# Two pairs of gate tiles at each layer end by seven half-size products, and another order of these products

## The chip, the core and the metric

The kernel runs on one core of a Trainium2 chip. The metric is the device time of one execution in microseconds (us), of the slowest core where there are several; here there is one. Lower is better. The engines are named as in the profile: PE multiplies matrices (PEld loads its weights), DVE is the vector engine, ACT the scalar engine, POOL is GpSimd, SP issues most DMAs. Each engine works through its own queue in the order in which the program writes it.

## The reference

A trunk of four layers works on 512 prompt rows and 8 sample rows together, 520 columns in the kernel. Every layer has another mixer (mLSTM, short convolution, dilated attention, pooling). The change touches what follows each mixer:

```python
def per_layer_embed(x, p, pe_w, pg_w):
    gate = jax.nn.sigmoid(x @ pg_w)
    return x + gate * (p.astype(x.dtype) @ pe_w)

x = x + mixer(rms_norm(x))          # ends with "@ w_out", the out projection
x = per_layer_embed(x, p[i], pe_w[i], pg_w[i])
```

Here x is 520 x 1024, pg_w is 1024 x 1024, p is 520 x 256. All is float32.

## The kernel before

**Numbers.** Activations lie transposed: eight tiles x[0..7] of 128 features x 520 columns. Every float32 operand is split into a high part, which PE takes as it is, and a low part, the rest; a product is high*high + low*high + high*low, so three matmuls for each block of 128 x 128 weights. `mm6` (L328) does one such block for all columns, in two halves of 256 and 264: six matmuls. `proj` (L410) does one output tile of 128 features: eight blocks, 48 matmuls.

**Weights.** A weight tile of 128 x 1024 is loaded by SP into one of four buffers `wf`. "high" copies it on ACT into one of four buffers `wh` (L255), "low" subtracts on DVE, wl = wf - wh (L264). For the names in MOVED (w_b and w_bo, the convolution's weights) the low part of a single tile, or of the first tile of a pair, is made otherwise: ACT writes -wh into `wl` (L260), and a DMA issued by POOL adds the weights from memory onto it (L262).

**Order.** Nothing is reordered at run time. `plan` (L60) lists the weight tiles in the order of use as Items with a cost in planned us (0.12 for a matmul). `due` (L114) goes through them once and gives each step a due time: "high" of an item is due when the earliest of the four `wh` buffers comes free, where an item holds its buffer from then until its begin plus cost (or plus `life`). While the program writes matmuls, `pump` (L289) moves a clock on by 0.72 for each `mm6` and 1.44 for each product of `seven`, and writes every weight step that has come due into its engine's queue right there. So the due time sets behind which other instructions of ACT, DVE and POOL a weight step stands. `item` (L308) sets the clock to the begin of the item that is taken.

**Seven products.** In the convolution two output tiles of 128 features for 520 columns are made together as a 2 x 2 block product by `seven` (L341): seven half-size products of 12 matmuls with 260 columns each, 84 in place of 96. For that POOL forms sums of the weights of a pair ("sum", four operations, L276 to L279), whose high and low parts ("hs", "ls", 512 wide) come from ACT and DVE, and sums of the activations are made once (`summed`, L568, POOL operations at L582 to L585). The products stand in PE's queue in the order 1 to 3, then what is still open of the pair before (`flush`), then 4 to 6; the seventh (`last`, L370) waits as the next thing to flush, in the next `seven` after its third product or in the next `proj` after its fourth block.

**Layer end.** `out_proj` (L613) adds the mixer's result to x[j], tile by tile, and splits x[j] into high and low parts (`xs`). Then `embed` (L632) runs over j = 0..7: 12 matmuls for p @ pe_w into `pe` (a weight tile w_pe serves four j), 48 for x @ pg_w into `pg` (w_pg), then the end of the tile: sigmoid on ACT (L647), two multiplications with `pe` (L649) and the addition to x[j] (L650) on DVE, the split for the next layer (ACT L469, DVE L470; in the last layer one copy on ACT), a square on ACT (L517) and its addition on DVE (L518). The weight steps that come due while a tile's matmuls are written follow in the queues. In planned us of this stage, tile j begins at 7.2 j, and a w_pe tile holds its buffer for 28.8. The last tile of the last layer is made in `final` (L661).

**Streams.** Work beside the matmuls is written as generators in streams; `tick`, every second block of a `proj`, moves each by one step.

Of the kernel before, what the change touches and what calls it, by code (L numbers as in the profile page):

```python
# [8 lines left out]
F32 = mybir.dt.float32  # L9
# [5 lines left out]
P = 128  # L15
# [24 lines left out]
NPLAIN = 3  # L40
HALF = T // 2
FBUFS, HBUFS, SBUFS = 4, 4, 4
MOVED = ("w_b", "w_bo")


# [14 lines left out]
def plan():  # L60

    out = []
    add = lambda *key, **kw: out.append(Item(key, **kw))

    def end(i, name, halves, begun=False):
        cs = range(2 if halves else 1)
        for c in cs:
            for j in range(2):
                if c or not begun:
                    last = c == len(cs) - 1 or i == 1  # L70
                    add(name, j, *([c] if halves else []), life=(2 - j) * 5.76 if last else None)
        for j in range(2, KD):
            for c in cs:
                add(name, j, *([c] if halves else []))
        for j in range(KD):
            if j % 4 == 0:
                add("w_pe", i, j // 4, cost=0, life=28.8)
            add("w_pg", i, j, cost=7.2)

    for hd in range(H):  # L80
        for j in (hd, 8 + hd, 16 + 2 * hd, 17 + 2 * hd, 32 + 2 * hd, 33 + 2 * hd):
            add("w_a", j)
    for j in range(16):
# [24 lines left out]
    for m in range(2):  # L108
        add("w_grp", 3, m)
    end(3, "w_do", True, True)  # L110
    return out


def due(items):  # L114
# [17 lines left out]
    for i, it in enumerate(items):  # L132
        it.begin = t
        if len(it.keys) == 1:
            ld = min(slots["wf"])
            sp = at(max(ld, take("wh", t + (it.life or it.cost))), i, "high")
            low = at(sp + 1.3, i, "low")
            at(take("wf", low + 2) - 0.01, i, "load")
        else:
            ld, ld2 = sorted(slots["wf"])[:2]  # L140
            one = at(max(ld, ld2, t - 12.8), i, "sum")
            h1 = at(max(ld, take("wh", t + 5.76), t - 14.4), i, "high")
            h2 = at(max(ld2, take("wh", t + 10.08), one + 6.6), i, "high2")
# [51 lines left out]
class Net:  # L195
# [47 lines left out]
    def make(self, i, op):  # L243
# [7 lines left out]
        new = lambda tag, n=1024, pool=None, dt=F32R: (pool or self.wp).tile([P, n], dt, tag=tag, name=self.nm(tag))  # L251

        def high(k, tag, n=1024, pool=None):
            t["h" + k] = new(tag, n, pool)
# [83 lines left out]
            mm(out[j], wl, a[0][:, PARTS[j]], start=False, stop=stop)  # L338
        self.pump(0.72)

    def seven(self, keys, B, dst, done):  # L341

# [51 lines left out]
        step()  # L394
        self.pend = last

# [216 lines left out]
    def out_proj(self, name, y, i, begun=None):  # L613

        nc = self.nc
        xs = []
        first = begun or self.proj_pair(name, y, 8 if i == 2 else 16)
        self.pt = [self.act() for _ in range(2)]
        for k in range(2):
            nc.sync.dma_start(self.pt[k], self.d["pT"][i, k])  # L620
        for j in range(KD):
# [8 lines left out]
        return xs  # L630

    def embed(self, i, xs):  # L632

        nc, d = self.nc, self.d
        hs, we = [], None
        g0 = C_NG + (i + 1) * KD
        for j in range(KD):
            if j % 4 == 0:
                we = self.weights("w_pe", i, j // 4)
# [3 lines left out]
            if i == 3 and j == KD - 1:  # L643
                return self.final(xs, pe, hs)
            pg = self.proj("w_pg", i, j, a=xs)
            sg = self.act()
            nc.scalar.activation(sg, pg, AF.Sigmoid)  # L647
            for u in range(2):
                nc.vector.tensor_mul(sg[:, PARTS[u]], self.part(pe, u), sg[:, PARTS[u]])  # L649
            nc.vector.tensor_add(self.x[j], self.x[j], sg)  # L650
            if i < 3:
                hs.append(self.split(self.x[j], self.col(g0 + j)))
            else:
                hs.append(self.act())
                nc.scalar.activation(hs[j], self.x[j], AF.Copy, scale=self.col(C_FG + j))
            self.square_in(j)
        self.sums = {} if i == 0 else None
        self.finish_norm(hs, g0, 3, *((4, 1), (2, 3), (0, 0))[i], sums=self.sums)
        return hs

    def final(self, xs, pe, xg):  # L661
# [8 lines left out]
        xg.append(self.act())  # L670
# [46 lines left out]
    def mlstm(self, h, lay):  # L717
# [3 lines left out]
        with ExitStack() as st:  # L721
# [53 lines left out]
            while main.gens or samp.gens:  # L775
                zs.append(self.scaled(self.proj("w_a", 48 + len(zs), a=h)))
        ex = lay.enter_context(tc.tile_pool(name="mly", bufs=16))
        self.streams = [self.gate]
        y = []
        for j, z in enumerate(zs):  # L780
# [271 lines left out]
    def conv(self, h, lay):  # L1052
# [4 lines left out]
        with ExitStack() as st:  # L1057
# [88 lines left out]
            self.look = 4  # L1146
            nc.sync.dma_start(d["o_conv_p"], po)
            nc.sync.dma_start(d["o_conv_s"], so)
        return y


    def attention(self, h, lay):
# [49 lines left out]
            gate()  # L1202

        self.finish = finish
        return y

    def rope(self, t, cs, out=None, keep=0):
# [237 lines left out]
    def pooling(self, h, lay):  # L1445
# [3 lines left out]
        with ExitStack() as st:  # L1449
# [22 lines left out]
            self.grouped(3, *last, y)  # L1472
            nc.sync.dma_start(d["o_pool_p"], pp)
            nc.sync.dma_start(d["o_pool_s"], sp[:, :, 1:16])
        return y, first

    def grouped(self, g, rr, zs, y):
# [40 lines left out]
    def run(self):  # L1518
# [32 lines left out]
        for i, (mixer, w) in enumerate(  # L1551
            ((self.mlstm, "w_ao"), (self.conv, "w_bo"), (self.attention, "w_co"), (self.pooling, "w_do"))
        ):
            with ExitStack() as lay:
# [4 lines left out]
            h = self.embed(i, xs)  # L1559


OUTS = {
# [124 lines left out]
```

## Time and profile before

| | us |
|---|---|
| median of 3 runs (2151.12 to 2155.94) | 2155.67 |
| the profiled execution | 2155.09 |
| its span, first to last instruction | 2153.3 |
| PE busy in the span | 2129.6 (99%) |
| DVE, ACT, POOL busy | 1383.3, 898.8, 395.2 |

The profile is one execution, the one of 2155.09 us. A matmul's record lasts longer than its place in the stream, since matmuls are pipelined: what counts is the distance between the starts of two. The granted clock of PE is 1.00 (2.4 GHz) in nearly the whole span.

### The profile page before, as it was taken

The page shows a single profiled execution, that of the slowest core. Times are in us where ns is not written, and L with a number is a line of the kernel's source. Part 1 is how long each engine was busy: PE and PEld are TensorE (multiplying, and loading weights), DVE is VectorE, ACT ScalarE, POOL GpSimd, SP SyncE. Part 2 cuts the span into 40 slices and gives each one's busy share as a digit, 9 for nine tenths or more (in the row PEclk, how much of TensorE's full clock was granted, in tenths as well). Part 3 has the DMA queues.
Part 4 walks back from the last instruction along what each step waited for, and adds up shares of the span by engine and source line. Part 5 has one row for each costly group of instructions (what it writes and reads, how often), then busy time and mean ns, then how long its engine had stood idle before and what let it go on. Part 6 is the DMA issues. An engine that isn't in the chain of part 4 may idle for free.

```text
span 2153.3 us, 42675 instructions
## 1 busy us (share of the span) xinstructions
PE 2129.6 (99%) x17560; PEld 2111.6 (98%) x17560; DVE 1383.3 (64%) x3064; ACT 898.8 (42%) x1434; POOL 395.2 (18%) x487
## 2 busy tenths in 40 slices
PE   8999999999999999999999999999999999999998
PEld 8999999999999999999999999999999999999998
DVE  7677767653565766751478787777867466666434
ACT  6544444432355554554333333333334342222223
POOL 1111110100035545521014223222220000000000
PEclk9999999999999999999999999999999999999999
DMA  4644454322257666678343555555544332323321
GB/s 164 193 177 143 154 182 165 99 95 93 89 140 165 159 169 164 157 198 188 88 136 120 162 193 190 185 173 165 199 169 156 98 114 93 98 90 99 119 79 50
DMA packets 112951, 305.22 MB, mean 142 GB/s; under 512 B 34260, under 2 KB 38612, under 8 KB 110708
## 3 DMA queue, kind: packets, MB, share of 16 engines
q1 hardware_dynamic: 104404, 272.54, 38.9%
q0 software_dynamic: 8208, 29.89, 7.8%
q8 instruction: 138, 2.26, 0.4%
q14 instruction: 57, 0.47, 0.1%
q10 hardware_dynamic: 144, 0.06, 0.0%
HBM read 279.63 MB, written 22.82 MB: 140 GB/s over the span
## 4 chain that ended last, share of the span: by engine, by line
PE 83%; DVE 6%; DMA 4%; issue 2%; ACT 2%; POOL 2%; SPq 0%; POOLq 0%; DVEq 0%; ACTq 0%
PE ps L334 23%; PE ps L338 23%; PE ps L336 23%; DMA wl<-w_b 2%; PE ax L1334 1%; PE ax L334 1%; PE ax L338 1%; PE ax L336 1%; DVE wl L264 1%; PE ax L364 1%; PE ax L362 1%; PE ax L363 1%; ACT wh L255 1%; PE ax L943 1%; PE ps L362 1%
## 5 line engine op out<-in xcount | busy, mean ns | idle before, releaser
L334 PE MATMUL ps<-hi,wh 128*128 128x256 f32 x4672 | 963.1, 287 | 1.8 <-DVE a L485 0.8
L338 PE MATMUL ps<-hi,wl 128*128 128x256 f32 x4672 | 939.5, 282 | 2.3 <-DMA wl<-w_b 2.3
L336 PE MATMUL ps<-lo,wh 128*128 128x256 f32 x4672 | 939.2, 282 | 0.1
L334 PEld LDWEIGHTS ps<-hi,wh 128*128 128x128 f32 x4672 | 725.8, 188 | 7.5 <-issue 1.4
L338 PEld LDWEIGHTS ps<-hi,wl 128*128 128x128 f32 x4672 | 723.4, 188 | 3.5 <-DMA wl<-w_b 3.3
L336 PEld LDWEIGHTS ps<-lo,wh 128*128 128x128 f32 x4672 | 725.3, 188 | 0.3 <-DVE lo L800 0.3
L264 DVE TENSOR_TENSOR wl<-wf,wh 128x1024 fp32r<-128x1024 f32 x287 | 364.2, 1272 | 167.3 <-ACT wh L255 163.8
L255 ACT ACTIVATE wh<-wf 128x1024 fp32r<-128x1024 f32 x344 | 360.8, 1053 | 157.2 <-issue 92.0
L1211 POOL TENSOR_TENSOR a<-a,a 32x520 f32<-32x520 f32 x48 | 68.9, 1436 | 296.1 <-ACT a L502 98.9
L627 DVE TENSOR_TENSOR x<-ps,x 128x520 f32<-128x520 f32 x32 | 22.4, 699 | 121.7 <-PE ps L338 121.6
L489 ACT ACTIVATE a<-a 128x520 f32<-128x520 f32 x42 | 26.8, 639 | 155.2 <-DVE a L485 155.1
L502 ACT ACTIVATE a<-ps 128x520 f32<-128x520 f32 x42 | 47.3, 1127 | 99.0 <-PE ps L338 72.5
L1212 POOL TENSOR_TENSOR a<-a,a 32x520 f32<-32x520 f32 x48 | 65.3, 1360 | 122.1 <-DVE a L1210 112.6
L466 ACT ACTIVATE hi<-x 128x520 fp32r<-128x520 f32 x32 | 20.5, 640 | 156.3 <-DVE x L627 156.3
L264 DVE TENSOR_TENSOR ls<-a,hs 128x512 fp32r<-128x512 f32 x57 | 65.4, 1158 | 12.1 <-ACT hs L255 11.9
L485 DVE TENSOR_TENSOR a<-ps,a 128x520 f32<-128x520 f32 x85 | 58.9, 693 | 20.8 <-PE ps L338 17.4
L649 DVE TENSOR_TENSOR a<-ax,a 128x256 f32<-128x256 f32 (+1 forms) x62 | 23.7, 424 | 72.5 <-ACT a L647 72.5
L1237 ACT ACTIVATE S<-S,nmx 128x128 f32<-128x128 f32 (+1 forms) x96 | 40.0, 417 | 65.8 <-DVE nmx L1234 65.5
L459 DVE CUSTOM_DVE_ANT_0 kc<-kc,qb 128x128 f32<-128x128 f32 (+1 forms) x192 | 54.3, 340 | 13.7 <-DMA kc<-kc 13.7
L262 POOL DMA_DIRECT2D wl<-w_b x41 | 36.3, 885 | 144.5 <-ACT wl L260 139.1
L260 ACT ACTIVATE wl<-wh 128x1024 fp32r<-128x1024 f32 x57 | 60.1, 1058 | 1.4
L1499 POOL COPY pool_p<-xpad 128x15 f32<-128x15 f32 x16 | 3.1, 196 | 300.7 <-DVE xpad L485 300.7
(344 smaller groups left out, 2924.4 us busy)
## 6 DMA issues: line engine op xcount, KB each, us to landing
wf<-w_c SPq DMA_DIRECT2D x80, 512.0 KB
wf<-w_a SPq DMA_DIRECT2D x64, 512.0 KB
wf<-w_b SPq DMA_DIRECT2D x64, 512.0 KB
wl<-w_b POOLq DMA_DIRECT2D x41, 512.0 KB, 7.1
wf<-w_pg SPq DMA_DIRECT2D x32, 512.0 KB
wf<-w_d SPq DMA_DIRECT2D x32, 512.0 KB
pb<-scr_p SPq DMA_DIRECT2D x8, 1292.0 KB
Ci<-C_in SPq DMA_DIRECT2D x16, 512.0 KB
```

Source lines behind the costliest of these rows:

```text
L255: nc.scalar.activation(t["h" + k], t["w" + k], AF.Copy)
L260: nc.scalar.activation(t["l1"], f(t["h1"]), AF.Copy, scale=-1.0)
L264: nc.vector.tensor_sub(t["l" + k], t["w" + k], f(t["h" + k]))
L334: mm(out[j], wh, a[0][:, PARTS[j]], start=start, stop=False)
L336: mm(out[j], wh, a[1][:, PARTS[j]], start=False, stop=False)
L338: mm(out[j], wl, a[0][:, PARTS[j]], start=False, stop=stop)
L362: mm(out, w[0][:, c], hi, start=start and k == 0, stop=False, **go)
L459: self.nc.vector.tensor_tensor_reduce(junk, a, b, 1.0, 0.0, ALU.mult, ALU.add, out)
L485: nc.vector.tensor_mul(dst[:, :T], ps, self.r)
L502: nc.scalar.activation(dst, split(ps), AF.Copy)
L1211: nc.gpsimd.tensor_mul(b[:32], t[:32], cs[0])
L1212: nc.gpsimd.tensor_mul(a[:32], a[:32], cs[1])
```

## The change

In every layer end, tiles 2 and 3, and tiles 5 and 6, of x @ pg_w are made by `seven`. Their weights are no MOVED names, so all their low parts come from DVE. Tile 3 (6) is ended inside `seven` behind its sixth product by the new hook `early`, tile 2 (5) after the seventh, as the hook `done`; the 12 matmuls of p @ pe_w of these two tiles move to just ahead of their ends. In the last layer what is open is flushed ahead of tile 7. The sums of activations that this needs are made by `crossed`, a stream of its own that starts as x[4..7] become ready: four subtractions on POOL, three steps of nothing, two copies on ACT, two subtractions on DVE, for each of four k; what is left of it is written out ahead of tile 2. `beside` opens the pools for it.

In `seven`, for the convolution too, the product with T4 (the sixth) comes fourth, ahead of the old fourth and fifth; the addition that makes the second tile then follows the addition u3.

In the planner: a pair of w_pg costs 12.96; a w_pe tile holds its buffer for 36.0; the first tile of any pair holds its `wh` until its begin plus 8.64 instead of 5.76; the low part of a single MOVED tile is due at once with its high part instead of 1.3 later.

```diff
+EPAIRS = (2, 5)
@@ plan
-                add("w_pe", i, j // 4, cost=0, life=28.8)
-            add("w_pg", i, j, cost=7.2)
+                add("w_pe", i, j // 4, cost=0, life=36.0)
+            if j in EPAIRS:
+                out.append(Item(("w_pg", i, j), ("w_pg", i, j + 1), cost=12.96))
+            elif j - 1 not in EPAIRS:
+                add("w_pg", i, j, cost=7.2)
@@ due
-            low = at(sp + 1.3, i, "low")
+            low = at(sp if it.moved else sp + 1.3, i, "low")
...
-            h1 = at(max(ld, take("wh", t + 5.76), t - 14.4), i, "high")
+            h1 = at(max(ld, take("wh", t + 8.64), t - 14.4), i, "high")
@@ seven
         self.flush()
+        product(r4, part("2", b), "T4", True)
+        step()
         product(r1, part("1", b), "21", False)
         nc.scalar.activation(dst[0][:, :HALF], r1, AF.Copy)
         step()
         product(r6, part("2", a), "T3", False)
         add(u3, r6, s1)
-        step()
-        product(r4, part("2", b), "T4", True)
         pair = lambda x, n: x.rearrange("p (u c) -> p u c", u=2)[:, :, :n]
         add(pair(dst[1], HALF), pair(v, HALF), u3.unsqueeze(1).broadcast_to([P, 2, HALF]))
+        if early:
+            early()
         step()
         self.pend = last
@@ out_proj
+            if j > 3:
+                self.side.gens.append(self.crossed(j - 4, xs))
@@ new
+    def crossed(self, k, xs):
...
+        sub(ta[:, a], t[:, b], t[:, a])
+        sub(ta[:, b], u[:, b], ta[:, a])
+        sub(tb[:, a], u[:, b], t[:, b])
+        sub(tb[:, b], u[:, a], ta[:, b])
+        for _ in range(4):
+            yield
...
+        for h, x in zip(hs, (ta, tb)):
+            nc.scalar.activation(h, x, AF.Copy)
+        yield
...
+            nc.vector.tensor_sub(l, x, h.bitcast(F32))
@@ embed
+        def two(j, we):
+            sg = self.act(), self.act()
+            end = lambda n: lambda: ends(j + n, part(we, j + n), sg[n], sg[n])
+            self.seven((("w_pg", i, j), ("w_pg", i, j + 1)), self.xsums, sg, end(0), end(1))
+
+        for j in range(KD):
+            if j % 4 == 0:
+                we = self.weights("w_pe", i, j // 4)
+            if j in EPAIRS:
+                self.side.drain()
+                two(j, we)
+            elif j - 1 not in EPAIRS:
+                if i == 3 and j == KD - 1:
+                    self.flush()
+                pe = part(we, j)
...
+                pg = self.proj("w_pg", i, j, a=xs)
+                ends(j, pe, self.act(), pg)
```

In this cut, `part(we, j)` writes the 12 matmuls of p @ pe_w, and `ends` is the end of a tile as described above.

## Rows read from the trace of the kernel before

**Rows 1.** The page: span, and engines with busy us, share and instructions.

```profile
span 2153.3 us, 42675 instructions
PE 2129.6 (99%) x17560; PEld 2111.6 (98%) x17560; DVE 1383.3 (64%) x3064; ACT 898.8 (42%) x1434; POOL 395.2 (18%) x487
```

**Rows 2.** Busy time by stretch: PE, PEld, DVE, ACT, POOL, clock, DMA; three layer ends.

```profile
545.00:603.00 58.00, 58.00 (x487) 58.00 (x486) 31.56 (x45) 23.75 (x33) 0.00 (x0) 1.00 0.25 76
...
1698.00:1756.00 58.00, 58.00 (x487) 58.00 (x486) 31.57 (x45) 24.01 (x33) 0.00 (x0) 1.00 0.26 82
2079.00:2137.00 58.00, 58.00 (x489) 58.00 (x488) 25.61 (x39) 22.50 (x32) 0.00 (x0) 1.00 0.09 28
```

**Rows 3.** Timeline of PE, layer 0: first matmuls of tiles 1 and 2 of `embed`.

```profile
552.36 0.40 PE L334 MATMUL ax<-hi,wh 128*128 128x256 f32 x2
...
559.53 0.40 PE L334 MATMUL ax<-hi,wh 128*128 128x256 f32 x2
```

**Rows 4.** Timeline of ACT there: start, us, operation, idle before it.

```profile
555.89 1.04 ACT L255 ACTIVATE wh<-wf 128x1024 fp32r<-128x1024 f32 x1
559.73 0.60 ACT L647 ACTIVATE a<-ps 128x520 f32<-128x520 f32 x1 [2.80 <-PE ps L338]
561.96 0.73 ACT L469 ACTIVATE hi<-x,cols 128x520 fp32r<-128x520 f32 x1 [1.62 <-DVE x L650]
562.59 0.62 ACT L517 ACTIVATE a<-x 128x520 f32<-128x520 f32 x1
563.12 1.04 ACT L255 ACTIVATE wh<-wf 128x1024 fp32r<-128x1024 f32 x1
```

**Rows 5.** Timeline of DVE there: the addition to x, and the low part.

```profile
561.16 0.70 DVE L650 TENSOR_TENSOR x<-x,a 128x520 f32<-128x520 f32 x1
...
564.20 1.23 DVE L264 TENSOR_TENSOR wl<-wf,wh 128x1024 fp32r<-128x1024 f32 x1
```

**Rows 6.** The convolution's u3 and pair additions: ns min/median/max, first and last start.

```profile
L389 DVE TENSOR_TENSOR a<-ax,a x19: 414/428/430, 681.1 to 934.1; 128x260 f32<-128x260 f32 x19
...
L393 DVE TENSOR_TENSOR a<-ps,a x19: 699/700/702, 682.5 to 935.6; 128x520 f32<-128x520 f32 x19
```

**Rows 7.** Low parts of weight sums: all of them, and one with POOL idle.

```profile
L264 DVE TENSOR_TENSOR ls<-a,hs 128x512 fp32r<-128x512 f32 x57 | 65.4, 1158 | 12.1 <-ACT hs L255 11.9
...
733.47 0.68 DVE L264 TENSOR_TENSOR ls<-a,hs 128x512 fp32r<-128x512 f32 x1
```

**Rows 8.** Timeline of POOL in the convolution: end of a sum, DMA issue, next sum.

```profile
699.45 1.74 POOL L279 TENSOR_TENSOR a<-wf,a 128x512 f32<-128x512 f32 x1
704.60 0.88 POOL L262 DMA_DIRECT2D wl<-w_b  x1 [3.41 <-ACT wl L260]
705.21 1.59 POOL L276 TENSOR_TENSOR a<-wf 128x512 f32<-128x512 f32 x1
...
709.74 1.74 POOL L279 TENSOR_TENSOR a<-wf,a 128x512 f32<-128x512 f32 x1
```

**Rows 9.** Timeline of ACT there: the copy s1 of the pair before.

```profile
705.57 0.39 ACT L377 ACTIVATE a<-ax 128x260 f32<-128x260 f32 x1 [0.85 <-PE ax L364]
```

**Rows 10.** POOL's weight DMAs in the convolution, and PE's waits on them (us, times, longest).

```profile
DMA to landing us min/median/max: 5.4/7.2/9.6
...
PE ps L338 <- DMA wl<-w_b: 2.3, 4, 0.6
```

**Rows 11.** Stretches in which PE rests (columns as rows 2).

```profile
1192.00:1194.00 2.00, 0.00 (x0) 0.00 (x0) 2.00 (x7) 0.00 (x0) 1.69 (x2) 1.00 0.27 109
...
2144.00:2147.00 3.00, 0.12 (x2) 0.00 (x0) 0.69 (x2) 0.69 (x1) 0.00 (x0) 1.00 0.80 251
2147.00:2150.00 3.00, 0.00 (x0) 0.00 (x0) 0.00 (x0) 0.00 (x0) 0.00 (x0) 0.72 0.83 277
```

**Rows 12.** Timeline of PE after its first wait of 5.12 us.

```profile
13.62 0.64 PE L336 MATMUL ps<-lo,a 128*64 128x256 f32 x2
14.06 0.64 PE L338 MATMUL ps<-hi,a 128*64 128x256 f32 x2
```

More of the change, by code (lines that the diff above doesn't have):

```diff
@@ L250, in make, with new @@
         f = lambda tile: tile.bitcast(F32)
-        new = lambda tag, n=1024, pool=None, dt=F32R: (pool or self.wp).tile([P, n], dt, tag=tag, name=self.nm(tag))
+        def new(tag, n=1024, pool=None):
+            if pool is self.ap:
+                return self.act(F32R, tag)[:, :n]
+            return (pool or self.wp).tile([P, n], F32R, tag=tag, name=self.nm(tag))
         def high(k, tag, n=1024, pool=None):
@@ L339, in mm6, with seven @@
         self.pump(0.72)
-    def seven(self, keys, B, dst, done):
+    def seven(self, keys, B, dst, done, early=None):
         nc = self.nc
@@ L617, in out_proj @@
         first = begun or self.proj_pair(name, y, 8 if i == 2 else 16)
+        self.side, self.xsums = Stream(1), {n: [] for n in ("11", "21", "22", "T1", "T2", "T3", "T4")}
+        self.streams = [*self.streams, self.side]
         self.pt = [self.act() for _ in range(2)]
@@ L628, in out_proj, with room, beside, part @@
             xs.append(self.split(self.x[j]))
+            if j > 3:
+                self.side.gens.append(self.crossed(j - 4, xs))
         self.look = 0
         return xs
+    def crossed(self, k, xs):
+        nc, B = self.nc, self.xsums
+        a, b = slice(0, HALF), slice(HALF, T)
+        sub = nc.gpsimd.tensor_sub
+        t, u = self.x[k], self.x[k + 4]
+        ta, tb = self.act(), self.act()
+        sub(ta[:, a], t[:, b], t[:, a])
[4 more added lines that the diff above has]
+            yield
+        def room(s):
+            self.spare -= 1
+            return self.act(F32R, s, self.ep if self.spare >= 0 else None)
+        hs = room("ha"), room("hb")
+        for h, x in zip(hs, (ta, tb)):
+            nc.scalar.activation(h, x, AF.Copy)
+        yield
+        ls = room("la"), room("lb")
+        for h, l, x in zip(hs, ls, (ta, tb)):
+            nc.vector.tensor_sub(l, x, h.bitcast(F32))
+        for n, (h, l), c in (("11", xs[k], a), ("21", xs[k + 4], a), ("22", xs[k + 4], b),
+                             ("T1", (hs[0], ls[0]), a), ("T2", (hs[0], ls[0]), b),
+                             ("T3", (hs[1], ls[1]), a), ("T4", (hs[1], ls[1]), b)):
+            B[n].append((h[:, c], l[:, c]))
+        yield
+    def beside(self, lay, n):
+        pool = lambda name, **kw: lay.enter_context(self.tc.tile_pool(name=self.nm(name), **kw))
+        self.sp = pool("ws", bufs=SBUFS)
+        self.ep, self.spare = pool("ep", bufs=n), n
     def embed(self, i, xs):
         nc, d = self.nc, self.d
-        hs, we = [], None
+        hs, we = [None] * KD, None
         g0 = C_NG + (i + 1) * KD
-        for j in range(KD):
-            if j % 4 == 0:
-                we = self.weights("w_pe", i, j // 4)
+        def part(we, j):
             pe = self.aux(), self.aux()
@@ L642, in embed, with ends @@
                 self.mm6(pe, we, ((j % 4) * 2 + k) * P, self.pt[k], k == 0, k == 1)
[L643 to L646, printed above, removed]
+            return pe
+        def ends(j, pe, sg, pg):
             nc.scalar.activation(sg, pg, AF.Sigmoid)
@@ L651, in embed @@
             if i < 3:
-                hs.append(self.split(self.x[j], self.col(g0 + j)))
+                hs[j] = self.split(self.x[j], self.col(g0 + j))
             else:
-                hs.append(self.act())
+                hs[j] = self.act()
                 nc.scalar.activation(hs[j], self.x[j], AF.Copy, scale=self.col(C_FG + j))
             self.square_in(j)
+        def two(j, we):
[12 more added lines that the diff above has]
+                pe = part(we, j)
+                if i == 3 and j == KD - 1:
+                    return self.final(xs, pe, hs)
+                pg = self.proj("w_pg", i, j, a=xs)
+                ends(j, pe, self.act(), pg)
         self.sums = {} if i == 0 else None
@@ L669, in final @@
         x, sg, sq = self.x[j], self.act(), self.act()
-        xg.append(self.act())
+        xg[j] = self.act()
         ch = lambda t, c: t[:, c * n : (c + 1) * n]
@@ L777, in mlstm @@
         ex = lay.enter_context(tc.tile_pool(name="mly", bufs=16))
+        self.beside(lay, 3)
         self.streams = [self.gate]
@@ L1148, in conv @@
             nc.sync.dma_start(d["o_conv_s"], so)
+        self.beside(lay, 3)
         return y
@@ L1204, in attention @@
         self.finish = finish
+        self.sp, self.ep, self.spare = self.ap, None, 0
         return y
@@ L1474, in pooling @@
             nc.sync.dma_start(d["o_pool_s"], sp[:, :, 1:16])
+        self.beside(lay, 10)
         return y, first
@@ L1558, in run @@
                 xs = self.out_proj(w, y, i, first)
-            h = self.embed(i, xs)
+                if i == 2:
+                    lay.close()
+                    self.beside(lay, 10)
+                h = self.embed(i, xs)
 OUTS = {
```

## The prediction

> **What bounds the kernel now.** I read the page first, then the busy time by stretch, then the timelines of single engines. The page says that PE is busy for 2129.6 of 2153.3 us [rows 1]. The stretches say it more sharply for the place of the change: in each layer end PE is busy for all of 58.00 us, ACT for 24 and DVE for 32 at most, POOL not at all [rows 2]. So every matmul taken out there is time, as long as PE does not have to wait instead; and PE waits when an operand is late. What makes operands late is the order in the queues of ACT and DVE.
>
> **What is taken out.** Tiles 1 and 2 begin 559.53 - 552.36 = 7.17 us apart, 60 matmuls, 0.1195 us each [rows 3]; this pitch holds for any 256 to 264 columns. Each pair saves 96 - 84 = 12 matmuls; two pairs in four layers are 96, so 96 x 0.1195 = 11.5 us. This is the whole gain: -11.5.
>
> **Where a weight step stands at a layer end.** The planner can be followed by hand, and the trace shows that it holds: in before, a copy to `wh` that is due when tile 2 begins stands directly behind tile 1's square, 563.12 after 562.59 [rows 4]. With the change, in planned us from the layer end's begin, the pair (2,3) begins at 14.4, the second w_pe and tile 4 at 27.36, the pair (5,6) at 34.56, tile 7 at 47.52. Four `wh` buffers: the first w_pe holds one until 36, w_pg 0 until 7.2, w_pg 1 until 14.4; the pair's first tile takes the fourth at 0 and holds it until 14.4 + 8.64 = 23.04; its second takes w_pg 0's and holds it until 24.48; the second w_pe takes w_pg 1's at 14.4 and keeps it. So w_pg 4's high part is due at 23.04, and the second tile of (5,6) is left with w_pg 4's own buffer, due at 34.56, the moment in which that pair begins.
>
> **First wait: tile 4.** Up to the fifth product the clock reaches 14.4 + 7.2 = 21.6; the 12 matmuls that `early` writes bring it to 23.04, where a step due at 23.04 is not yet written (pump asks for 0.01 more); then come the sigmoid, copy and square of tile 3; only the pump behind them writes w_pg 4's high and low. So the copy stands behind the whole end of tile 3. From the moment at which PE starts what follows the sixth product: u3 starts 0.20 later (as the sigmoid at 559.73 after 559.53 [rows 3, 4]); it takes 0.43, a hand-over some 0.1, and the pair addition 0.70 [rows 6], until 1.42; sigmoid at 1.46. From a sigmoid's start to the start of the copy behind the square it is 563.12 - 559.73 = 3.39, and to the start of the low part on DVE 564.20 - 559.73 = 4.47 [rows 4, 5]. So the copy runs from 4.85 to 5.89, the low part from 5.93 to 7.16. PE meanwhile has 12 matmuls of tile 3 and 12 of tile 4, 2.87, and then wants the high part: it waits 3.1, until 5.95; four matmuls on, at 6.43, it wants the low part and waits 0.8 more, until 7.22. Sum 3.9 for each layer, **+15.5**. What is moved to ahead of this place, the matmuls of p @ pe_w, is in the 2.87. Queued behind the late copy on ACT are the parts of (5,6); none is wanted before tile 4 is done.
>
> **Second wait: the fourth product of (5,6).** T4 in fourth place wants the pair's second tile after three products, 36 x 0.1195 = 4.31; nothing is open to be flushed there, since tile 4 has flushed. Its high part stands behind the end of tile 4, and on DVE the low part of s4 (0.68, [rows 7]) and the end of tile 2 stand ahead of that: tile 2 is ended 24 matmuls before tile 4, so its last addition on DVE ends some 0.9 after tile 4's last matmul, the low part of s4 at 1.66, and only then tile 4's multiplications start; in before they start right after the sigmoid, at 0.20 + 0.60 and a hand-over, 0.84. The chain is late by 0.8: copy 0.2 + 0.8 + 3.39 = 4.4 to 5.45, low part until 0.2 + 0.8 + 4.47 + 1.23 = 6.7. PE waits 1.2 for the high part, does two matmuls, and waits 1.0 for the low part: 2.2 for each layer, **+8.8**. Bounds: 1.4 if tile 2's end costs nothing; 2.7 if the low part of s4 takes the mean of 1.158 [rows 7].
>
> **Layer 2 alone.** Its out projection has half the blocks, so the crossed sums get 12 steps in it and 8 in tiles 0 and 1, of the 24 needed. The fourth one's copies are written out behind the end of tile 1: two copies of 520 columns (0.62 by the square's row, [rows 4]) run from 0.20 + 3.39 = 3.6 into the pair to 4.8, the first low part on DVE (0.70, [rows 5]) from some 4.6, behind tile 1's last addition, to 5.3; the second product wants it in its last block, at 1.43 + 1.08 + 0.12 = 2.6. **+2.7**, between 0 and 3.5. In the other layers the sums end before tile 2.
>
> **What hides.** The crossed sums on POOL, four pair sums and the added ACT and DVE work lie beside 58 us of PE in which POOL rests, ACT works 24 and DVE 32 [rows 2]; added are, per layer, some 10 us on ACT (six hs and eight crossed copies of 0.62, four of 0.39) and 15 on DVE (six ls of 0.68 to 1.16, eight crossed of 0.70, four more additions of 0.43 to 0.70 a pair), part of them in the out projection. Uncovered, they cost only where named above. A pair's sum takes 709.74 + 1.74 - 705.21 = 6.3 us on POOL [rows 8] and is due 12.8 before its pair.
>
> **The convolution.** Holding `wh` until +8.64 moves the first high part of a pair behind two pairs from -14.4 to -11.52 of its begin, so its low part's DMA issue (-10.2) falls behind that pair's own sum (-12.8) in POOL's queue; in before it stood ahead [rows 8]. The pair before begins 1.44 + 0.20 ahead of its s1 at 705.57 [rows 9], at 703.94, this one 84 matmuls later, at 713.98, and wants the low part at 714.22. The sum can start when the former one ends, at 699.45 + 1.74 = 701.2 [rows 8], and ends at 707.5; the issue then lands 7.2 later, at 714.7 [rows 10]. That is 0.5 in each of six periods, **+3.0**; landings of 5.4 and 9.6 [rows 10] make it 0 and 17. Two edits there have no row: single MOVED tiles (high part due 2.88 later where they take a pair's buffer, low part 1.3 earlier), and T4 in fourth place (its weights are due 4.9 ahead of the pair; the pair addition ends 0.5 later, with 24 matmuls or more to the flush). I take 0 for both together; bounds -2, if today's waits of 2.3 on such DMAs go, and +4, if each of the four [rows 10] grows by 1.
>
> **The sum** against the profiled execution: 2155.09 - 11.5 + 15.5 + 8.8 + 2.7 + 3.0 = **2173.6**. That execution is 0.6 below the median of 2155.67, which changes nothing.
>
> **The skill against the trace.** DVE's low parts of 512 columns take 0.68 with POOL idle and 1.16 on average [rows 7], and most of them lie beside POOL's sums. The Trainium skill, GPSIMD Engine Reference, section 1, says that POOL shares its SBUF interfaces with VectorE and that instructions with two SBUF inputs contend; the trace agrees. By that rule the chains above are too short if (5,6)'s sum runs beside them. The sum needs only its loads, which are free early, and ends near the sixth product, so I leave the chains as they are; beside it, the addition (0.70) and the low part (1.23) would grow by 1158/680, some 1.3 for each first wait, 5 us in all: it is in the upper end.
>
> **Rivals.** (1) *The matmuls saved are the whole story*: the copies are hidden because ACT reaches them early (another order in the queue than I read), and the convolution stays: 2155.09 - 11.5 = 2143.6. For it: ACT has idle time of 2.80 ahead of a sigmoid [rows 4]. Against it: that idle time lies in front of the sigmoid, and ACT does not let a later copy pass. It decides at one point: if w_pg 4's copy stands ahead of tile 3's sigmoid. (2) *Only part of the waits*: the first is halved (the copy behind the sigmoid only, its low part not behind tile 3's addition), the second and layer 2's gone: 2155.09 - 11.5 + 7.8 + 3.0 = 2154.4, no change. (3) *The waits also cost PE's clock.* At the kernel's end the granted clock is 1.00 in the 3 us in which PE goes idle and 0.72 in the next 3, and in the rest of 2 us in mid-kernel it stays at 1.00 [rows 11]. After the kernel's first wait of 5.12 us PE's matmuls still stand (14.06 - 13.62) / 2 = 0.22 apart 9 us later [rows 12]. The 3.1 and 0.8 us of the first wait are near the rests that kept the clock, so I give it little; if four stretches like the first followed, each 9 us at 0.22 for 0.12, they would cost 9 x (1 - 0.1195 / 0.22) = 4.1 each and give 2173.6 + 16.4 = 2190. The Trainium skill, TensorE: Matmul & The Clock Gate, Part 1, says that an idle PE falls to half rate and rises again after work; by that rule each wait would be followed by such a stretch. (4) *The DMA of the convolution lands late throughout* (9.6): 14 more, 2187.
>
> **How the numbers follow.** Chances: the forecast with its bounds 0.75, (1) 0.10, (2) 0.07, (3) 0.04, (4) 0.04. Within the forecast: low with 1.4 for the second wait, 0 for layer 2 and 0 for the convolution: 2155.09 - 11.5 + 15.5 + 5.6 = 2164.7; high with 2.7, 3.5, 5 for POOL and 6 for the convolution: 2155.09 - 11.5 + 15.5 + 10.8 + 3.5 + 5 + 6 = 2184.4. The range must leave out (1) and the far end of (3); I set it from 2159 to 2187. A measurement of this kernel tells 0.3% (6.5 us) from no change. Faster by more than that: (1), 0.10. Within: (2), 0.07. Slower: the rest, 0.83.
>
> **What the changed kernel's profile would show.** Right: at each layer end, PE waits of 3 and 0.8 us ahead of the first block of a `proj`, released by ACT `wh` and DVE `wl`, behind a sigmoid, copy and square; two waits near 1 us in a fourth product; one wait of over 2 us on `la` in layer 2 only; PE's count of matmuls lower by 96; in the convolution, sums directly behind sums on POOL and DMA issues after them. Wrong: PE busy for all of a layer end of 54.6 us; a granted clock under 1.00 in a layer end; POOL waits that hold up the sums; waits for activation buffers, of which the change holds up to 16 more, and which the trace of before cannot show.

## The result, and the profile after

The changed kernel takes 2201.99 us, the kernel before 2154.73 beside it on the same chip: a ratio of 1.0223, 95% interval 1.0211 to 1.0236. That is slower by 47 us, where 18 were forecast. The profiled execution has a span of 2201.7 us at a mean granted clock of 0.988 (before: 2153.3 and 0.999). Its page has PE with 96 matmuls fewer than [rows 1], as planned, but 97% busy where it was 99%, and POOL at 519 us for 395:

```profile
span 2201.7 us, 42826 instructions
PE 2143.5 (97%) x17464; PEld 2120.3 (96%) x17464; DVE 1461.3 (66%) x3152; ACT 933.8 (42%) x1506; POOL 519.3 (24%) x583
```

The table gives the stages' spans in us, read from the timelines: a layer end runs from the start of the out projection's last addition to x to the first reciprocal of the norm behind it, the fourth to the end of the kernel; "between" is what lies ahead of each.

| kernel | layer ends 0, 1, 2, 3 | between | time (median) |
|---|---|---|---|
| before | 64.5, 64.6, 64.6, 74.0 | 545.4, 432.3, 591.2, 316.6 | 2154.73 |
| after | 76.3, 75.1, 77.4, 83.1 | 544.8, 433.6, 595.0, 316.5 | 2201.99 |

44.1 of the 48.4 us lie in the layer ends, of which 61.6, 61.7, 61.7 and 71.1 would be left if the saved matmuls were all. What PE waited for (us in total, times, longest), in the whole kernel:

```profile
PE ax L369 <- DVE a L387: 10.1, 3, 4.0
PE ps L341 <- ACT wh L262: 10.1, 4, 2.9
...
PE ax L370 <- DVE la L669: 3.3, 1, 3.3
PE ps L371 <- DVE wl L271: 3.0, 4, 0.8
PE ps L369 <- ACT wh L262: 3.0, 4, 0.8
...
PE ax L369 <- ACT ha L665: 2.1, 1, 2.1
PE ps L345 <- DMA wl<-w_b: 1.7, 3, 1.1
PE ps L345 <- DVE wl L271: 1.6, 3, 0.5
```

L369 to L371 are the three matmuls of a block in `seven`, L341 to L345 those in `mm6`; L262 copies to `wh`, L271 makes the low part. In order: the sixth product, since the change the one with T3, waiting for the addition u2 (L387; not forecast); tile 4 waiting for its high part, and in the last row for its low part (the first wait); two rows for layer 2's crossed sums; two for the fourth product of (5, 6) (the second wait). The convolution's waits on its DMAs are 1.7 for 2.3 in [rows 10]. The layer ends' rows sum to 33.2 us, where [rows 2] had none.

The first wait, on ACT in layer 0: the copies to `wh` stand behind tile 3's split and square, as forecast (start, us, operation, idle before it).

```profile
577.02 0.73 ACT L478 ACTIVATE hi<-x,cols 128x520 fp32r<-128x520 f32 x1 [1.63 <-DVE x L698]
577.66 0.62 ACT L526 ACTIVATE a<-x 128x520 f32<-128x520 f32 x1
578.18 1.99 ACT L262 ACTIVATE wh<-wf 128x1024 fp32r<-128x1024 f32 x2
```

The unforecast one, on DVE in the same layer, and on POOL beside it the first and the last operation of the sum of (5, 6):

```profile
562.98 1.51 DVE L479 SCALAR_TENSOR_TENSOR lo<-x,cols,hi 128x520 fp32r<-128x520 f32 x1 [0.80 <-ACT hi L478]
564.42 1.81 DVE L527 TENSOR_TENSOR a<-a,a 128x520 f32<-128x520 f32 x1
566.15 1.75 DVE L271 TENSOR_TENSOR ls<-a,hs 128x512 fp32r<-128x512 f32 x1
567.83 2.28 DVE L271 TENSOR_TENSOR wl<-wf,wh 128x1024 fp32r<-128x1024 f32 x1
570.02 0.42 DVE L387 TENSOR_TENSOR a<-ax,a 128x260 f32<-128x260 f32 x1
```
```profile
562.65 1.29 POOL L283 TENSOR_TENSOR a<-wf 128x512 f32<-128x512 f32 x1 [8.28 <-DMA wf<-w_pg]
...
567.31 1.71 POOL L286 TENSOR_TENSOR a<-wf,a 128x512 f32<-128x512 f32 x1
```

PE has the matmul before at 566.19 and then stands until u2 (L387) has read the bank that the sixth product goes on in; behind it matmuls come 0.22 apart, not 0.12:

```profile
566.19 0.28 PE L371 MATMUL ax<-hi,wl 128*128 128x260 f32 x1
570.50 0.59 PE L369 MATMUL ax<-hb,wh 128*128 128x260 f32 x1 [4.03 <-DVE a L387]
570.88 0.42 PE L370 MATMUL ax<-lb,wh 128*128 128x260 f32 x1
571.10 0.42 PE L371 MATMUL ax<-hb,wl 128*128 128x260 f32 x1
```

The stretches show it as the granted clock, the third number from the end (before it the engines' busy time, behind it DMA share and GB/s), after each of three groups of waits in this layer end:

```profile
569.00:571.00 2.00, 0.50 (x2) 0.51 (x3) 1.44 (x2) 0.00 (x0) 0.02 (x1) 0.81 0.00 0
571.00:573.00 2.00, 2.00 (x11) 2.00 (x10) 0.00 (x0) 0.00 (x0) 0.00 (x0) 0.50 0.80 256
...
581.00:583.00 2.00, 2.00 (x11) 2.00 (x11) 1.22 (x2) 0.21 (x1) 0.00 (x0) 0.50 0.53 205
...
595.00:597.00 2.00, 0.66 (x3) 0.46 (x4) 1.90 (x3) 1.75 (x3) 0.00 (x0) 1.00 0.00 0
597.00:599.00 2.00, 2.00 (x12) 2.00 (x13) 1.26 (x2) 0.00 (x0) 0.00 (x0) 0.63 0.44 141
599.00:601.00 2.00, 2.00 (x12) 2.00 (x11) 0.00 (x0) 0.00 (x0) 0.00 (x0) 0.51 0.88 250
```

### The profile page after: what moved, and what is told of

Its sections match the earlier page's. It is cut to its first block, busy times and chain, and to the rows that moved or that the text cites. A ratio compares the mean times of both kernels' runs of the same rounds, so it can differ in the third digit from the quotient of the medians.

```text
span 2201.7 us, 42826 instructions
## 1 busy us (share of the span) xinstructions
PE 2143.5 (97%) x17464; PEld 2120.3 (96%) x17464; DVE 1461.3 (66%) x3152; ACT 933.8 (42%) x1506; POOL 519.3 (24%) x583
## 4 chain that ended last, share of the span: by engine, by line
PE 82%; DVE 8%; ACT 3%; issue 3%; DMA 2%; POOL 1%; SPq 0%; ACTq 0%; DVEq 0%; POOLq 0%
PE ps L341 21%; PE ps L345 21%; PE ps L343 21%; DVE wl L271 2%; DMA wl<-w_b 2%; PE ax L369 2%; PE ax L371 1%; PE ax L370 1%; PE ps L371 1%; PE ps L369 1%; PE ps L370 1%; PE ax L1405 1%; ACT wh L262 1%; DVE x L698 1%; PE ax L343 1%
## 5 line engine op out<-in xcount | busy, mean ns | idle before, releaser
L341 PE MATMUL ps<-hi,wh 128*128 128x256 f32 x4416 | 913.9, 288 | 13.1 <-ACT wh L262 10.1
L345 PE MATMUL ps<-hi,wl 128*128 128x256 f32 x4416 | 891.2, 283 | 3.3 <-DMA wl<-w_b 1.7
L343 PE MATMUL ps<-lo,wh 128*128 128x256 f32 x4416 | 890.4, 283 | 0.4 <-DVE lo L1205 0.2
L341 PEld LDWEIGHTS ps<-hi,wh 128*128 128x128 f32 x4416 | 689.0, 189 | 19.8 <-ACT wh L262 10.9
L345 PEld LDWEIGHTS ps<-hi,wl 128*128 128x128 f32 x4416 | 686.4, 189 | 5.1 <-DVE wl L271 2.5
L343 PEld LDWEIGHTS ps<-lo,wh 128*128 128x128 f32 x4416 | 687.2, 189 | 0.8 <-DVE lo L1205 0.4
L271 DVE TENSOR_TENSOR wl<-wf,wh 128x1024 fp32r<-128x1024 f32 x287 | 379.5, 1326 | 158.4 <-ACT wh L262 156.2
L262 ACT ACTIVATE wh<-wf 128x1024 fp32r<-128x1024 f32 x344 | 360.4, 1053 | 148.4 <-issue 87.5
L511 ACT ACTIVATE a<-ps 128x520 f32<-128x520 f32 x42 | 47.5, 1130 | 101.4 <-PE ps L345 75.1
L271 DVE TENSOR_TENSOR ls<-a,hs 128x512 fp32r<-128x512 f32 x81 | 80.3, 998 | 5.6 <-ACT hs L262 5.6
L494 DVE TENSOR_TENSOR a<-ps,a 128x520 f32<-128x520 f32 x85 | 58.9, 693 | 19.7 <-PE ps L345 16.4
L369 PE MATMUL ax<-hi,wh 128*128 128x260 f32 x216 | 62.8, 291 | 0.0
L370 PE MATMUL ax<-lo,wh 128*128 128x260 f32 x216 | 62.3, 288 | 0.0
L371 PE MATMUL ax<-hi,wl 128*128 128x260 f32 x216 | 62.3, 288 | 0.1
```

What stands on the lines that cost most here:

```text
L262: nc.scalar.activation(t["h" + k], t["w" + k], AF.Copy)
L271: nc.vector.tensor_sub(t["l" + k], t["w" + k], f(t["h" + k]))
L341: mm(out[j], wh, a[0][:, PARTS[j]], start=start, stop=False)
L343: mm(out[j], wh, a[1][:, PARTS[j]], start=False, stop=False)
L369: mm(out, w[0][:, c], hi, start=start and k == 0, stop=False, **go)
L370: mm(out, w[0][:, c], lo, start=False, stop=False, **go)
```

## The experiments

The theory: waits that come from the order in the queues of ACT and DVE, one that comes from POOL's sum beside DVE, and a clock that falls after them. Each ratio is to the kernel before, with its 95% interval.

**Is the low clock a cost of its own, and does it come from the idle time?** Idle products fill the waits; for tile 4 in this form:

```diff
+        if name == "w_pg" and idx[-1] == 4:
+            for _ in range(22):
+                mm = self.nc.tensor.matmul
+                mm(self.part(ps, 0), self.pw[:, :P], a[0][0][:, PARTS[0]], start=True, stop=True)
```

> The changed kernel with idle products put into PE's waits: 32, 30, 0 and 17 matmuls ahead of the sixth product of (2, 3) in layers 0 to 3, 43 inside the second product of layer 2, 22 ahead of tile 4's gate, 6 ahead of the fourth product of (5, 6). They write where a later product starts afresh, so the result is the same; at 0.12 us each they are a little shorter than the waits they stand in, and no wait is taken away. The waits of the changed kernel come to about 33 us, its conv and attention cost about 5 more, seven products give back 11.5, and 48.4 are to be explained: some 21 us are left. If these are the clock's, which falls because PE stood still: 2182 (2177 to 2188), a mean granted clock of 0.996 or more. If they are not, and the lower clock comes from something else than the idle time: 2202 (2198 to 2210), clock 0.988.

2190.91 us, 1.0165 (1.015 to 1.018), mean granted clock 0.998: 11 us back, between the two numbers. The layer ends took 72.0, 72.1, 72.5 and 80.8, together 14.4 less than after; the stretches outside took 3.7 more in this one profile. The same stretches as above:

```profile
571.00:573.00 2.00, 1.77 (x14) 1.56 (x14) 0.77 (x2) 0.00 (x0) 0.00 (x0) 1.00 0.05 16
...
581.00:583.00 2.00, 2.00 (x20) 2.00 (x19) 1.29 (x2) 0.28 (x1) 0.00 (x0) 1.00 0.65 197
...
597.00:599.00 2.00, 2.00 (x19) 2.00 (x18) 0.00 (x0) 0.39 (x1) 0.00 (x0) 1.00 1.02 250
599.00:601.00 2.00, 2.00 (x19) 2.00 (x19) 1.11 (x2) 0.00 (x0) 0.00 (x0) 1.00 0.58 229
```

At 597 the DMA engines move as much as in the changed kernel at 599, 250 GB/s, and the clock is full: so it was the idle time and not the transfers. The Trainium skill, TensorE: Matmul & The Clock Gate, Part 1, says that work must precede full rate and that an idle PE loses it; these rows agree. That the clock gives back 11 to 14 and not 21 has a reason that layer 0 shows: its waits are 8.9 by the list (4.0, 2.8, 0.5, 0.8, 0.8), but by the starts of matmuls in the filled kernel the same five gaps, with the first matmul behind each, come to 10.5, which is all of 72.0 - 61.6. In this layer a wait thus costs some 0.3 more than is listed, 1.5 in all: 64.5 - 2.9 + 8.9 + 1.5 = 72.0, the filled kernel's layer 0, and the 4.3 from there to the changed kernel's 76.3 are what the filling took away, the clock's.

**The first wait: ACT's queue.** One number lets the copy be issued ahead of tile 3's end.

```diff
-            h1 = at(max(ld, take("wh", t + 8.64), t - 14.4), i, "high")
+            h1 = at(max(ld, take("wh", t + (7.2 if it.keys[0][0] == "w_pg" else 8.64)), t - 14.4), i, "high")
```

> One number of the planner: the first weight of a gate pair counts as read until 7.2 us after the pair's begin instead of 8.64, so the copy for tile 4's high part is issued within tile 3's embedding product, ahead of tile 3's sigmoid on ACT and not behind tile 3's end. If the first wait is one of ACT's queue: the 2.9 + 0.5 us that PE waits at tile 4's begin fall to about 1 in each layer, 9 to 10 us; with the clock that the waits cost it (a third of some 21 us) 2183 to 2188. If waits count alone and the clock has another cause: 2192. If the copy is late for another reason, its DMA or its buffer: 2202.

2184.55 us, 1.0134 (1.0118 to 1.0149), 17 us less, as the theory had it. The copy runs at 567.31, and the sigmoid of tile 3 8 us behind it, and tile 4's high part has left the list of waits (0.2 is left on the low part):

```profile
567.31 1.05 ACT L262 ACTIVATE wh<-wf 128x1024 fp32r<-128x1024 f32 x1
575.22 0.64 ACT L695 ACTIVATE a<-a 128x520 f32<-128x520 f32 x1 [6.87 <-DVE a L400]
```

**The wait for u2: the queue or POOL?** Three kernels. The first was to move u2 ahead of the two low parts, and did not: all steps of a pair are made at its begin, whatever their due time, so the two only changed places.

```diff
-            low = at(sp if it.moved else sp + 1.3, i, "low")
+            low = at(sp if it.moved else sp + (6 if it.keys[0][0] == "w_pe" and it.keys[0][2] else 1.3), i, "low")
-            ... ("4", t - 2.0, t + 17.3)):
+            ... ("4", t + (6 if it.keys[0][0] == "w_pg" else -2), t + 17.3)):
```

> Two due times of the planner: the last low part of a gate pair, and the low part of the second embedding weight, are made some 8 and 5 us later, so that the sum u2 stands ahead of both in DVE's queue. Nothing of POOL is changed. If u2 is late by what stands ahead of it in the queue: the wait of the sixth product in layers 0, 1 and 3 (4.0, 3.8 and 2.2) falls under 0.5, 10 us, and with the clock's share of some 6 about 2186 (2183 to 2193). If its own operation is held up by POOL, whatever stands ahead: 2202 (2198 to 2204), the wait within 1 us of what it was.

2196.77 us, 1.0192 (1.0175 to 1.0209); PE still waits 8.5 for u2. It says nothing on the question. The second leaves DVE's order alone and moves POOL's sum:

```diff
+        self.junk = self.cp.tile([P, 1], F32, name="junk")
...
         elif op == "sum":
...
+            if it.keys[0][0] == "w_pg" and it.keys[0][2] == 5:
+                nc.gpsimd.tensor_copy(self.junk, self.hold)
...
         add(u2, r6, s1)
+        self.hold = u2[:, 0:1]
```

> DVE's order is as in the changed kernel, but POOL makes the weight sum of (5, 6) only after u2 of (2, 3): one copy of one column of u2 stands ahead of that sum on POOL. If DVE's operations ahead of u2 are stretched by POOL's sum (1.75 us for the low part of a half weight, where 0.68 was seen alone, 2.28 for a whole one, 1.23 alone): the wait for u2 falls from 4.0, 3.8 and 2.2 to at most 1 each, and the time to about 2188 (2184 to 2194). If the order alone makes u2 late: no change, 2202 (2198 to 2204).

2188.51 us, 1.0154 (1.0138 to 1.0169). The five operations of DVE, in the same order, with POOL idle until u2:

```profile
564.20 0.76 DVE L483 SCALAR_TENSOR_TENSOR lo<-x,cols,hi 128x520 fp32r<-128x520 f32 x1 [0.80 <-ACT hi L482]
564.88 0.69 DVE L531 TENSOR_TENSOR a<-a,a 128x520 f32<-128x520 f32 x1
565.49 0.68 DVE L272 TENSOR_TENSOR ls<-a,hs 128x512 fp32r<-128x512 f32 x1
566.09 1.22 DVE L272 TENSOR_TENSOR wl<-wf,wh 128x1024 fp32r<-128x1024 f32 x1
567.22 0.42 DVE L390 TENSOR_TENSOR a<-ax,a 128x260 f32<-128x260 f32 x1
```

From the first to u2 it is 3.0 us for 7.0. The wait for u2 is gone from the list, and layer 2's wait for `la` fell from 3.3 to 0.6, though nothing of the crossed sums was touched. But the sum now runs beside tile 3's end, where the addition to x takes 1.40 for 0.70, and tile 4's wait went from 10.1 to 13.7: what was held up moved. The third keeps the due times of the first and really puts u2 ahead, with POOL's sum where it was:

```diff
-        while any((j, op) not in self.made for _, _, j, op in self.ops[self.begun :] if j == i):
+        while any((j, op) not in self.made for _, _, j, op in self.ops[self.begun :] if j == i and not (keys[0][0] == "w_pg" and op[-1] == "4")):
```

> What u2_first meant to do and did not (there the two low parts only changed places, both still ahead of u2): here the pair's last part is not made at the pair's begin but when it is due, so u2 stands behind tile 1's end alone in DVE's queue, with POOL's sum as in the changed kernel. By the chain of layer 0: u2 at 566.6 where it was at 570.0, so the sixth product waits under 0.5; but the two low parts, 2.28 and 1.75 beside POOL's sum, now stand ahead of u3, which starts at 571.0 where it started at 573.5, and tile 4 starts 5.8 after u3 as before. So the sixth product's wait goes (10.1 to under 2), tile 4's grows from 2.9 to 5 or more, and the time falls by 2.5 us in three layers and a little clock, to 2191 (2187 to 2196). If order were all, with nothing late behind: 2186.

2187.91 us, 1.0154 (1.0137 to 1.0172), 14 less where 11 were expected (6 to 15). Again the wait for u2 is gone and again tile 4 waits longer, and so, in two layers, do the matmuls of p @ pe_w, for u3 (L398):

```profile
PE ps L341 <- ACT wh L262: 13.7, 4, 3.7
...
PE ax L341 <- DVE a L398: 1.3, 2, 0.6
```

So both are causes: two operations too many ahead of u2, and each at about twice its time. Taking either away is enough to end this wait.

**The fourth place.** The old order of products in the layer ends alone.

```diff
-        product(r4, part("2", b), "T4", True)
-        step()
+        if not early:
+            product(r4, part("2", b), "T4", True)
+            step()
...
+        if early:
+            step()
+            product(r4, part("2", b), "T4", True)
```

> In the layer ends alone the product T4 goes back behind the one that reads u2; the convolution keeps the new order. If the fourth place makes the second wait: the 0.8 + 0.8 us at (5, 6) vanish in every layer, 6.4 with their clock some 9; but the product that waits for u2 comes 1.44 earlier, so that wait grows from 4.0, 3.8 and 2.2 to 5.4, 5.2 and 3.6 and appears in layer 2, and (2, 3) frees its last weight no earlier than before. Sum: 2198 (2193 to 2203). If the fourth place costs nothing and helps u2 alone: 2206 or more.

2199.82 us, 1.021 (1.019 to 1.023): the sum was right, its terms were not. The second wait is gone, but the wait for u2 is 10.3, not longer; instead the product that follows into r1 waits for ACT to have read it, seven times:

```profile
PE ax L369 <- DVE a L387: 10.3, 3, 4.0
...
PE ax L369 <- ACT a L384: 8.0, 7, 1.3
```

The fourth place hides these 8.0 and pays 6.0 for it.

**All waits together.** To the edits of copy_first and hold_sum (or u2_ahead) two are added:

```diff
-        self.side, self.xsums = Stream(1), ...
+        self.side, self.xsums = Stream(2 if i == 2 else 1), ...
...
                 pg = self.proj("w_pg", i, j, a=xs)
+                if j == 4:
+                    self.pump()
```

> Four edits together: tile 4's copy ahead of tile 3's end (copy_first), POOL's sum held until u2 (hold_sum), the copy of the second weight of (5, 6) issued ahead of tile 4's end and not behind it, and in layer 2 two steps of the crossed sums for every one. If these four waits and the clock that they cost are all that the change loses at the layer ends: 2155 less 11.5 for the 96 matmuls, and 1.3 to 4 more in the convolution and the attention: 2146 (2142 to 2152). If the waits only move on to other work: 2165 or more. If the smaller products run slower than counted: 2155 to 2160 with no wait left.

> The same four edits, but u2 is moved ahead in DVE's queue (as u2_ahead) in place of holding POOL's sum. Lows and adds of the stretch still run beside POOL's sum at about twice their time. If the places in the queues are what matters: within 3 us of fix_hold. If DVE's time beside POOL is what matters: u3 is late, tile 3's end with it, and a wait for DVE or ACT stays at tile 4 or behind it: 4 to 12 us above fix_hold.

2171.13 us, 1.0075 (1.0058 to 1.0092), and 2168.29, 1.0064 (1.004 to 1.0088): 25 and 22 above the number expected, on the side of the rival that the waits only move on (2165 or more), and within 3 of each other: with the places in the queues mended it made no difference whether POOL's sum ran beside DVE's work ahead of u2 or behind it. One large wait is left, and it has grown from 0.8 to 2.9 (3.6 in fix_hold):

```profile
PE ps L371 <- DVE wl L271: 11.1, 4, 2.9
```

The copy on ACT is ahead of tile 4's sigmoid, so tile 4's end is later, and the low part still stands behind that end on DVE. The next two put the low part ahead too:

```diff
                 if j == 4:
+                    self.clock += 1.4
                     self.pump()
```

> fix_ahead, with the low part of the second weight of (5, 6) put ahead of tile 4's end on DVE as well, and not the copy on ACT alone. In fix_ahead the copy came earlier and PE still waited 2.9 at the fourth product of (5, 6) in each layer, now for the low part, which stood behind tile 4's five operations in DVE's queue. If that queue is the second wait: it goes, 11.1 and some 3 to 4 of clock, and 2154 is left (2150 to 2158). If tile 4's end, pushed back, stops PE at another place: 2160 to 2168.

> The same edit upon fix_hold, where the wait for that low part was 3.6 in each layer, 14.3 together. If DVE's queue is the wait: 2171 less 14.3 and 3 to 4 of clock: 2153 (2149 to 2158), the same as fix2_ahead within 3. If the low part is late by POOL's sum, which here runs later than in fix2_ahead: a wait of 1 to 2 stays and the time is 4 to 8 above fix2_ahead.

2152.82 us, 0.9989 (0.998 to 0.9999), and 2154.66, 1.0 (0.9991 to 1.0009). Both are where they were expected, with clocks of 0.999 and 0.998; the wait is out of the list. What the layer ends have left in fix2_ahead, 63.7, 63.7, 61.5 and 72.0 long:

```profile
PE ax L369 <- ACT a L384: 1.9, 4, 0.6
...
PE ax L341 <- DVE a L398: 1.3, 2, 0.7
```

**The convolution.** Its share of the change alone in the kernel before, and fix2_ahead without it:

```diff
-            low = at(sp + 1.3, i, "low")
+            low = at(sp if it.moved else sp + 1.3, i, "low")
-            h1 = at(max(ld, take("wh", t + 5.76), t - 14.4), i, "high")
+            h1 = at(max(ld, take("wh", t + 8.64), t - 14.4), i, "high")
+        product(r4, part("2", b), "T4", True)
+        step()
         product(r1, part("1", b), "21", False)
...
-        step()
-        product(r4, part("2", b), "T4", True)
```

> The kernel before with the convolution's share of the change alone: T4 in fourth place, its first weight's buffer kept longer, the low part that ACT and a transfer of POOL make issued at the same due time as the copy; the layer ends are as before. By the stage's span, 432.3 before and 433.6 to 434 after: 2156 (2154 to 2158). By the prediction's 0.5 us for each of six late transfers: 2157.7. If the fourth place takes waits away here as it does at the layer ends: 2150. The attention took 591.2 before and 593.5 to 596 in every kernel with the new layer ends: 591 here if the layer ends bring that, 594 or more if the convolution does.

> fix2_ahead with the convolution as in the kernel before. By the stage spans 1 to 2 us below fix2_ahead, 2152.5 (2149 to 2156). If nothing of the convolution's change costs time: equal to fix2_ahead within 1.

2158.57 us, 1.0015 (1.0005 to 1.0024): 3.2 slower by the ratio, above the 2156 expected and nearest to the rival of 2157.7. And 2149.56 us, 0.9971 (0.9959 to 0.9983): 3.3 faster than fix2_ahead, where 1 to 2 were expected, and 0.3% faster than the kernel before, the best of all here. Both say that the convolution's share costs about 3. Where is not settled: its stage took 432.5 in conv_only for 432.3, and 429.9 without the share for 433.4 with it, while the stage ahead of it, in which the kernels hardly differ, ranged from 543.9 to 546.1 over the profiles. The waits that were forecast, on the transferred low part of a pair's first tile, are hardly there: none is listed in the changed kernel and none in fix2_ahead, and one in conv_only:

```profile
PE ax L364 <- DMA wl<-w_b: 0.9, 1, 0.9
```

All listed waits on such transfers, those of single tiles with them, are 1.7 in the changed kernel and 1.4 in conv_only for 2.3 in the kernel before, but 1.8 in fix2_ahead for none in fix2_ahead_conv.

The attention took 592.9 in conv_only, for 591.2 before and 593.2 to 596.3 with new layer ends. These 1.7 are the clock's. In every kernel PE rests there once for 2.3 to 2.4 us (the rest in [rows 11]). Behind it the granted clock stays at 1.00 in the kernel before (first line) and falls in the changed kernel (the others), which loses 1.7 us by it:

```profile
1194.00:1196.00 2.00, 1.89 (x15) 1.82 (x16) 2.00 (x6) 0.00 (x0) 0.00 (x0) 1.00 0.41 106
...
1218.00:1220.00 2.00, 1.23 (x5) 1.11 (x6) 2.00 (x6) 0.00 (x0) 0.35 (x1) 0.69 0.23 29
1220.00:1222.00 2.00, 2.00 (x11) 2.00 (x11) 2.00 (x5) 0.00 (x0) 0.80 (x1) 0.50 0.83 324
```

It falls there in 8 of the 14 profiles, conv_only among them, and not in 6; what decides it, no run here shows. So 1.7 of the 3.5 us by which conv_only's profile is longer lie in the attention and not in the convolution. The other 2.1 of the changed kernel's 3.8 there were not taken apart.

## Why the prediction was wrong

The direction was right, the size too small: 2173.6 forecast, 2187 the upper end, 2202 measured. By its own steps:

- **Saved matmuls, -11.5**: PE's count is lower by 96, and fix2_ahead shows the gain once the waits are gone: layer ends 6.7 shorter in sum, 11.5 less the 3.2 still listed and their restarts.
- **First wait, 15.5 in sum**: right in mechanism, place and size. Listed are 2.8 and 0.5 in layer 0 for 3.1 and 0.8; by the starts of matmuls, as the sum was made, the two gaps in the filled kernel are 4.0 with their restarts, for 3.9 in the forecast. copy_first took it away by the point named under rival (1).
- **Second wait, 8.8**: listed 0.8 and 0.8 for 1.2 and 1.0, with restarts 2.1 for 2.2. Right. To move one half of it is not enough: with the copy alone ahead (fix_ahead) the low part was waited for by 2.9, with both ahead (fix2_ahead) neither is listed.
- **Layer 2, +2.7**: right in kind, too small: 3.3 and 2.1. The chain was made with DVE's unstretched times; with POOL's sum held, 2.1 and 0.6 were left, which is 2.7.
- **The convolution, +3.0**: the number agrees, the mechanism is not shown. The transfer's issue stands directly behind a pair's own sum, as forecast against [rows 8], and two pairs of kernels give 3.2 and 3.3. But the 0.5 us of waiting in each of six periods is not there: the listed waits on a pair's transfer are none in the changed kernel and in fix2_ahead and 0.9 in conv_only. That the number came out is luck as far as these traces go. The places on POOL:

```profile
710.60 1.31 POOL L286 TENSOR_TENSOR a<-wf,a 128x512 f32<-128x512 f32 x1
711.85 1.76 POOL L283 TENSOR_TENSOR a<-wf 128x512 f32<-128x512 f32 x1
...
717.53 1.75 POOL L286 TENSOR_TENSOR a<-wf,a 128x512 f32<-128x512 f32 x1
719.21 0.89 POOL L269 DMA_DIRECT2D wl<-w_b  x1
```

- **Step that failed first: what hides.** "Uncovered, they cost only where named above", and the sum of (5, 6), said to end near the sixth product, was counted at nothing in the chains. Its end was right, 569.0. But it runs beside the whole chain that leads to u2, which the prediction never followed: u2 was an operation with no place in a queue. 10.1 us listed, 10.6 or so as gaps. The rule named there (the Trainium skill, GPSIMD Engine Reference, section 1) was applied to the first wait, where POOL rests, and not to the stretch in which POOL works; these runs agree with it at 0.69 against 1.81 and 1.22 against 2.28.
- **Step that failed second: rival (3), given 0.04.** Its price, 16.4, was near: 14.4 by the layer ends, 11.1 by the time. In part that is luck, since it assumed one slow stretch of 9 us in each layer and the profile has two or three of some 3 to 7 us; and at [rows 12], from which the 9 us come, the profile gives the granted clock as 1.00, so they were read from the distance of matmuls alone. The chance was wrong. It took the clock's behaviour at rests of 2 and 3 us [rows 11] as a reason that waits of 3.1 and 0.8 would leave it alone. The rest of 2 us did leave it alone in that profile, but this was one outcome of two: the same rest cost the clock in 8 of 14 profiles, as shown above. In the changed kernel 0.81 and 0.76 us of waiting, within some 2 us, were followed by 4 us at 0.63 and 0.51. This too was not so each time: of the 12 such pairs of waits at (5, 6) in the changed kernel, copy_first and hold_sum, 7 were followed by a lower clock.

With the measured terms put in, the sum is 2173.6 + 10.6 + 14.4 + 2.7 (layer 2) = 2201.3. It was made afterwards, and in it the convolution's 3.0 stands for the 4.3 by which everything outside the layer ends took longer.

## What to carry to other kernels

For each operand of a moved or shortened product, write down which operations stand ahead of its producer in that engine's queue, the small additions that free a bank included, and price those operations as they run beside whatever POOL does at that time. A wait of some us that is new to a stretch with a busy PE should be priced with the slow matmuls that can follow it: here 11.1 to 14.4 us on 33.2 us of listed waits. One rest after which the clock stayed up does not show that the next one is free. And a copy moved ahead in one engine's queue gains only if its partner on the next engine moves too.

## What the runs showed of the hardware

- DVE's operations with two inputs in SBUF took 1.51 to 2.28 us beside POOL's sum in the changed kernel where they took 0.68 to 1.22 with POOL idle in hold_sum, a factor of 1.9 to 2.6. POOL's operations of 512 columns took 1.65 to 1.72 beside them, and 1.28 to 1.30 where DVE was idle in the changed kernel, a factor of 1.3. u2, which reads PSUM, took 0.42 with POOL idle (hold_sum) and no more beside POOL's sum (u2_ahead; DVE, then POOL):

```profile
566.58 0.41 DVE L387 TENSOR_TENSOR a<-ax,a 128x260 f32<-128x260 f32 x1
566.06 1.75 POOL L285 TENSOR_TENSOR wf<-wf,wf 128x512 f32<-128x512 f32 x1
```

- In layer 0 of the changed kernel PE's granted clock was 0.50 or 0.51 (the level of 1.2 GHz) for 2 to 4 us after waits of 4.0, of 2.8 + 0.5 and of 0.8 + 0.8, and 1.00 throughout where other products stood in the same places. Waits of up to 1.4 in the layer ends, one at a time (fix2_hold), were followed by 1.00.
- The same wait does not always cost the clock: PE's one rest of 2.3 to 2.4 us in the attention was followed by 0.50 in 8 of 14 profiles and by 1.00 in 6.
- A wait cost PE about 0.3 us beyond its listed length, in the starts of the matmuls around it: 8.9 us listed for five waits in layer 0 were 10.5 by the starts.
